# Layer A's attention on Trainium2: the value products of near, block and selected keys in one batch per tile and group

## The chip, the cores and the metric

The kernel runs on one core of a Trainium2 chip. The metric is the device time of one execution in microseconds. Three runs of the kernel before took 2791.73, 2793.88 and 2795.78 us; the median is 2793.88 us. Times inside the kernel come from one profiled execution, counted from the start of its span. PE is TensorE, DVE is VectorE, ACT is ScalarE, POOL is GpSimd, SP is SyncE, which issues DMAs.

## The reference, cut to what matters

The program is a two-layer decoder trunk on 1024 tokens of width 1024. Layer A's attention has 16 heads in 4 groups; the 4 heads of a group share their keys and values. Each query attends three sets of keys, and the three results are added under gates:

```python
s = einsum('bsgrd,bngd->bgrsn', q, k_cmp) * scale          # 63 compressed blocks
p, denom, _ = masked_softmax(s + bias_c, dist_c >= 0)
p_cmp = p / maximum(denom, 1e-30)
o_cmp = einsum('bgrsn,bngd->bsgrd', p_cmp, v_cmp)
_, sel_idx = top_k(score, 8)                               # 8 of 16 key blocks, from p_cmp
...
o_sel = einsum('bcgrk,bgckd->bcgrd', p_sel / den, vg)      # the selected blocks alone
o_win, _ = banded_attention(q, kwn, vwn, 255, 1, rel_bias) # the last 256 keys
o = g[..., 0:1] * o_cmp + g[..., 1:2] * o_sel + g[..., 2:3] * o_win
```

Everything is float32. Layer B's dilated attention, the projections and the feed-forward parts are not edited, apart from one call in layer B whose arguments become fewer.

## The kernel before, in words

The stage in question is layer A's attention; its value products stand in the trace from 286 to 673 us of 2792. Its unit of work is one group `g` (4 of them) and one tile `t` of 128 queries (8 of them): 32 units, taken group by group. For one unit:

- `near_scores` (called `a` for two heads and `b` for the other two) multiplies queries by the keys of the tile and of two tiles before it and by the 63 compressed keys (line 758), and DVE adds the bias, takes the minimum and moves the scores from PSUM to SBUF (lines 759 and 761, weights in the tiles `P2` and `pc`). `block_weights` (`c`) turns the compressed scores into weights and, for t of 4 and more, into the mask of selected blocks, which `block_mask` (`m`) turns with PE (line 813).
- `far_scores` (`f`, `g`, two heads each) does the same for all keys up to the tile (lines 845 to 847), in tiles `P1` of 128 x 2 x 1024 numbers, of which there are 4. `exponentials` runs the exponential on ACT (line 738), the reciprocal on DVE (740) and the scaling by sum and gate on POOL (742).
- `near_values` (`n`) and `far_values` (`v`) multiply weights by values. A weight tile has the queries on its partitions, so PE turns it first: `turned` makes four 128 x 128 transposes into a PSUM bank `pt` (line 353; three such banks) and ACT or DVE, in turn, copies the bank to a tile `pT` (line 356; 5 such tiles). A product then has 64 columns of values as PE's weights and 256 turned columns as the moving side; two heads' products go to two halves of PE's columns (line 390). For 128 keys ("a block") that is two products, which the profile shows as four records, since each float32 product runs as two.

The helper `values` does this for a list of blocks in batches of at most 3: it turns up to 3 blocks, and then does their products, last block first, with `after(prev)` so that the products stand behind the last transpose on PE. `near_values` calls it for 1 to 3 near blocks and appends the product of the compressed keys to the batch; `far_values` calls it for the t + 1 blocks of the selected keys, in 1 to 3 batches. Both add into the same half bank `o` in PSUM, which `po_` hands from one to the other; DVE then copies it to `oT` (line 860).

`turn(i)` sets the order of steps in the source: a(i+2), m(i), f(i), v(i-1), b(i+2), c(i+2), n(i), g(i). The language's scheduler reorders from there what does not depend on each other, so that on PE scores of later units stand between transposes and products of earlier ones.

Of the kernel before, what the change touches and what calls it, by code (L numbers as in the profile page):

```python
# [10 lines left out]
F32 = mybir.dt.float32  # L11
# [118 lines left out]
def trunk(ctx, tc, I, out):  # L130
    nc = tc.nc
# [74 lines left out]
    def after(prev):  # L206
        return tc.issue_after(prev.ins) if prev is not None else ExitStack()
# [141 lines left out]
    def turned(p, heads, copy):  # L349

        ps = bank("pt")
        for i, h in enumerate(heads):
            prev = nc.tensor.transpose(ps[:, i * 128:(i + 1) * 128], h, ident)  # L353
        w = len(heads) * 128
        t = p.tile([128, 512], F32, name="pT", bufs=5)
        copy(t[:, :w], ps[:, :w])  # L356
        return t, prev

# [7 lines left out]
            self.i += 1  # L366
            return self.parts[(self.i - 1) % len(self.parts)]

    copies = [0]

    def values(p, po, Ps, vs, first, last, behind=None, more=None):

        nb = len(vs)
        ends = [nb * (i + 1) // -(-nb // 3) for i in range(-(-nb // 3))]
        for lo, hi in zip([0] + ends, ends):
            ts = []
            for b in range(lo, hi):
                copies[0] += 1  # L380
                t, prev = turned(p, [Ps[hp][:, e, b * 128:(b + 1) * 128] for e in range(2) for hp in range(2)],
                                 (nc.scalar.copy, nc.vector.tensor_copy)[copies[0] % 2])
                ts.append(t)
            ops = [(vs[b], vs[b], ts[b - lo][:, :256], ts[b - lo][:, 256:]) for b in reversed(range(lo, hi))]
            if more is not None and lo == 0:
                ops.append(more)
            for i, (*v, ta, tb) in enumerate(ops):
                with after(prev), after(behind if lo == i == 0 else None):
                    for e, t in enumerate((ta, tb)):
                        mm = nc.tensor.matmul(po[64 * e:64 * e + 64, :256], v[e], t, start=first and lo == i == 0,  # L390
                                              stop=last and hi == nb and i == len(ops) - 1, skip_group_check=True)
                prev = mm
        return prev

    def pipelined(jobs, lag=1):

# [26 lines left out]
    vc = ares.tile([128, G, 128], F32, name="vc")  # L423
# [4 lines left out]
    with ExitStack() as c:  # L428
# [62 lines left out]
        with ExitStack() as c2:  # L491
# [14 lines left out]
            first = [xget(t) for t in range(4)]  # L506
# [12 lines left out]
            prev = norm_to_hT(np_, xget, g_mix[0], *hT, 4, 4)  # L519
# [147 lines left out]
        grp = {}  # L667
# [55 lines left out]

        pcs = [kP.tile([128, 4, 64], F32, name=f"pc{i}") for i in range(3)]
        units = [(g, t) for g in range(G) for t in range(NT)]
        po_, blocks_, weights = {}, {}, {}
        first_banks = Turns(("cmp0", "cmp1"))
        score_bank = lambda: psum["s"].tile([128, 512], F32, name="s", bufs=4) if "s" in psum else bank(first_banks())
        gt = lambda g, t, br, h0, n: gates[:, t, 12 * g + 3 * h0 + br:12 * g + 3 * (h0 + n):3]
# [47 lines left out]
        def block_weights(g, t):  # L777
            pc, pv, mx, nv = blocks_[g, t]
            dn = kP.tile([128, 4], F32, name="cd", bufs=3)
            for hh in range(4):  # L780
                nc.scalar.activation(pc[:, hh, :nv], pc[:, hh, :nv], AF.Exp, bias=mx[:, hh:hh + 1], scale=-1.0,
                                     accum_out=dn[:, hh:hh + 1])
            nc.vector.tensor_scalar(dn, dn, 1e-30, None, op0=OP.max)
            nc.vector.reciprocal(dn, dn)
            if t == 0:
                nc.vector.tensor_scalar(dn, dn, crow, None, op0=OP.mult)
            dg = kP.tile([128, 4], F32, name="dg", bufs=3)
            nc.vector.tensor_mul(dg, dn, gt(g, t, 0, 0, 4))
            if t >= 4:
                pn = wk.tile([128, 4, 64], F32, name="pn", bufs=2)  # L790
                nc.gpsimd.tensor_mul(pn[:, :, :nv], pv, dn[:].unsqueeze(2).to_broadcast([128, 4, nv]))
            nc.gpsimd.tensor_mul(pv, pv, dg[:].unsqueeze(2).to_broadcast([128, 4, nv]))
            if t >= 4:
                a4 = wk.tile([128, 68], F32, name="a4", bufs=2)
                nc.gpsimd.memset(a4, 0.0)
                nc.vector.tensor_reduce(a4[:, 1:1 + nv], pn[:, :, :nv].rearrange("p h n -> p n h"), axis=AX.X,
                                        op=OP.add)
                sc = wk.tile([128, 16], F32, name="sc", bufs=2)
                nc.vector.tensor_reduce(sc, a4[:, 1:65].rearrange("p (j i) -> p j i", i=4), axis=AX.X, op=OP.add)
                nc.vector.tensor_add(sc, sc, a4[:, 0:64].rearrange("p (j i) -> p j i", i=4)[:, :, 0])  # L800
                nc.vector.tensor_add(sc, sc, force[:, t, :])
                m8 = wk.tile([128, 8], F32, name="m8", bufs=2)
                nc.vector.max(out=m8, in_=sc)
                s2_ = wk.tile([128, 16], F32, name="s2", bufs=2)
                nc.vector.match_replace(out=s2_, in_to_replace=m8, in_values=sc, imm_value=-3e38)
                mk = wk.tile([128, 16], F32, name="mk", bufs=2)
                nc.vector.tensor_scalar(mk, s2_, -2e38, BIG, op0=OP.is_gt, op1=OP.mult)
                grp["mask", g, t] = mk
# [8 lines left out]
        def near_values(g, t):  # L817
            pc = blocks_[g, t][0]
            pT, _ = turned(wk, [pc[:, 2 * c:2 * c + 2, :] for c in range(2)], nc.vector.tensor_copy)
            po = po_[g, t] = outs()  # L820
            k0 = max(t - 2, 0)
            ends[0] = values(wk, po, grp["P2", g, t], [grp["V", 1, g, b // 4][:, b % 4, :] for b in range(k0, t + 1)],
                             True, False, ends[0], (vc[:, g, :64], vc[:, g, 64:], pT[:, :256], pT[:, :256]))

        def far_scores(g, t, hp):

            n = 128 * (t + 1)
            P = weights[1, hp] = wk.tile([128, 2, 1024], F32, name="P1", bufs=4)
            mm = kP.tile([128, 2], F32, name="m", bufs=8)
            masked = t >= 4  # L830
            kh, kl = grp["K", g]
# [22 lines left out]
                grp["P1", g, t] = weights[1, 0], weights[1, 1]  # L854

        def far_values(g, t):
            po = po_[g, t]
            ends[0] = values(wk, po, grp["P1", g, t], [grp["V", 0, g, b // 4][:, b % 4, :] for b in range(t + 1)],
                             False, True)
            nc.vector.tensor_copy(oT[:, 2 * g:2 * g + 2, tok(t)], po.rearrange("p (c q) -> p c q", q=128))  # L860

        def loads(g, t):
# [51 lines left out]
    with ExitStack() as c:  # L914
        kB = pool(c, "aB")
        wk = pool(c, "aw")
# [759 lines left out]
    oT_ctx, bctx = ExitStack(), ExitStack()  # L1676
    oT = pool(oT_ctx, "oTb", "left").tile([128, KC, S], F32, name="oTb")
    bC, bA = pool(bctx, "bC", "right"), pool(bctx, "bA", "right")
    with ExitStack() as c:
        wk = pool(c, "bw")  # L1680
        bB = pool(c, "bB")
# [75 lines left out]
        def unit(key, hp, stats, slot, score, bias, n, blocks, dst):  # L1757
# [15 lines left out]
            def back():  # L1773
                if hp == 0:
                    return
                po = outs()
                behind[0] = values(wk, po, both, blocks, True, True, behind[0])
                nc.vector.tensor_copy(dst, po[:, :256].rearrange("p (c q) -> p c q", q=128))
            return back

# [184 lines left out]
```

## Time and profile before

| what | value |
|---|---|
| median of the runs | 2793.88 us |
| span of the profiled execution | 2792.1 us |
| PE busy over the span | 2738.9 us (98%) |
| DVE, ACT, POOL busy over the span | 79%, 51%, 50% |
| layer A's attention, 286 to 672 us: PE busy | 376.31 of 386 us |
| there: DVE, ACT, POOL busy | 316.45, 279.32, 217.59 us |
| granted TensorE clock there | 1.00 |

The profiled execution's span is 1.8 us under the median of the runs and inside their spread. Its busy figures are sums of the stretches in which an engine has an instruction under way. Matmuls are pipelined and their ends are modelled, so two starts on PE tell more than a duration and a gap. A wait of an engine is put down to the semaphore that came last.

### The profile page before, as it was taken

The page shows a single profiled execution, that of the slowest core. Times are in us where ns is not written, and L with a number is a line of the kernel's source. Part 1 is how long each engine was busy: PE and PEld are TensorE (multiplying, and loading weights), DVE is VectorE, ACT ScalarE, POOL GpSimd, SP SyncE. Part 2 cuts the span into 40 slices and gives each one's busy share as a digit, 9 for nine tenths or more (in the row PEclk, how much of TensorE's full clock was granted, in tenths as well). Part 3 has the DMA queues.
Part 4 walks back from the last instruction along what each step waited for, and adds up shares of the span by engine and source line. Part 5 has one row for each costly group of instructions (what it writes and reads, how often), then busy time and mean ns, then how long its engine had stood idle before and what let it go on. Part 6 is the DMA issues. An engine that isn't in the chain of part 4 may idle for free.

```text
span 2792.1 us, 43025 instructions
## 1 busy us (share of the span) xinstructions
PE 2738.9 (98%) x14494; PEld 2218.9 (79%) x14494; DVE 2214.7 (79%) x4527; ACT 1426.8 (51%) x3171; POOL 1402.8 (50%) x1454
## 2 busy tenths in 40 slices
PE   9999999999999999999999999999999999999997
PEld 8988676776788888888778888777778888888886
DVE  5453888887889899989875677688898888888987
ACT  5531777775644343333454444577756433343434
POOL 3135655552465566565457787110014756655652
PEclk9999999999999999999999999999999999999999
DMA  8669443224122322232224555786341211112112
GB/s 237 218 196 298 133 128 105 68 62 159 35 76 69 83 65 68 62 77 62 84 80 116 167 156 159 242 257 187 114 174 44 74 58 57 49 57 61 54 42 83
DMA packets 292924, 315.13 MB, mean 113 GB/s; under 512 B 50428, under 2 KB 229677, under 8 KB 292704
## 3 DMA queue, kind: packets, MB, share of 16 engines
q1 hardware_dynamic: 272240, 249.40, 30.5%
q0 software_dynamic: 20464, 62.99, 7.4%
q8 instruction: 115, 1.88, 0.3%
q14 instruction: 105, 0.86, 0.1%
HBM read 243.96 MB, written 81.95 MB: 117 GB/s over the span
## 4 chain that ended last, share of the span: by engine, by line
PE 85%; DVE 6%; ACT 2%; issue 2%; DMA 2%; POOL 1%; SPq 1%; POOLq 0%; DVEq 0%; ACTq 0%
PE ux L1161 18%; PE uy L1161 15%; PE dx L993 8%; PE o L390 7%; PE pt L353 6%; PE dr L993 6%; PE dr L1161 4%; PE mm L230 3%; PE mm L229 3%; PE mm L231 3%; PE s L758 1%; DVE pl L954 1%; PE s L846 1%; PE s L1808 1%; PE s L845 1%
## 5 line engine op out<-in xcount | busy, mean ns | idle before, releaser
L954 DVE TENSOR_TENSOR pl<-oT,ph 128x512 fp32r<-128x512 f32 x340 | 340.2, 1018 | 72.3 <-PE dr L993 17.4
L953 ACT ACTIVATE ph<-oT 128x512 fp32r<-128x512 f32 x346 | 211.8, 628 | 215.6 <-PE ux L1161 53.3
L954 DVE TENSOR_TENSOR pl<-oTb,ph 128x512 fp32r<-128x512 f32 x232 | 214.7, 948 | 27.2 <-PE dr L993 17.4
L953 ACT ACTIVATE ph<-oTb 128x512 fp32r<-128x512 f32 x238 | 145.5, 628 | 168.7 <-PE ux L1161 53.4
L353 PE MATMUL pt<-ident,P 128*128 128x128 f32 x1536 | 228.0, 278 | 3.3 <-DVE pT L356 1.9
L742 POOL TENSOR_SCALAR P<-P,sm,gates 128x384 f32<-128x384 f32 (+7 forms) x256 | 183.2, 727 | 79.3 <-DVE sm L740 54.8
L353 PEld LDWEIGHTS pt<-ident,P 128*128 128x128 f32 x1536 | 172.9, 140 | 61.8 <-issue 43.0
L998 DVE TENSOR_TENSOR xrfx<-xrfx,dr 128x512 f32<-128x512 f32 x320 | 204.2, 679 | 17.8 <-PE dr L993 17.7
L1354 POOL TENSOR_TENSOR oT<-oT,gffn 128x512 f32<-128x512 f32 x92 | 118.9, 1303 | 196.0 <-DMA oT<-in_ffn_w_up_dram 127.7
L998 DVE TENSOR_TENSOR xrfx<-xrfx,dx 128x512 f32<-128x512 f32 x320 | 204.5, 678 | 2.2 <-PE dx L993 2.2
L738 ACT ACTIVATE P<-P,m 128x384 f32<-128x384 f32 (+7 forms) x256 | 171.1, 670 | 36.0 <-DVE m L851 14.9
L356 DVE COPY pT<-pt 128x512 f32<-128x512 f32 (+1 forms) x224 | 143.2, 648 | 44.5 <-PE pt L353 39.8
L1354 POOL TENSOR_TENSOR oTb<-oTb,gffn 128x512 f32<-128x512 f32 x92 | 111.8, 1226 | 130.8 <-DMA oTb<-in_ffn_w_up_dram 79.0
L356 ACT COPY pT<-pt 128x512 f32<-128x512 f32 x192 | 110.1, 578 | 103.8 <-PE pt L353 100.8
L390 PE MATMUL o<-pT,V 128*64 128x256 f32 x1200 | 160.7, 391 | 2.3 <-ACT pT L356 1.5
L1770 ACT ACTIVATE P<-P,st 128x384 f32<-128x384 f32 (+2 forms) x256 | 139.6, 548 | 32.3 <-DVE st L1765 30.4
L1765 DVE CUSTOM_DVE_ANT_0 P<-s,T 128x384 f32<-128x384 f32 (+2 forms) x256 | 112.9, 478 | 10.5 <-PE pt L353 3.0
L390 PEld LDWEIGHTS o<-pT,V 128*64 128x64 f32 x1200 | 73.6, 136 | 51.8 <-issue 9.9
L993 PE MATMUL dx<-ph 128*128 128x512 f32 x320 | 107.5, 390 | 0.8 <-ACT ph L953 0.8
L993 PE MATMUL dx<-ph,pl 128*128 128x512 f32 x320 | 107.0, 389 | 0.0
L847 DVE CUSTOM_DVE_ANT_0 P<-s,T 128x128 f32<-128x128 f32 (+3 forms) x192 | 99.5, 550 | 8.1 <-PE s L846 7.8
L230 PE MATMUL mm<-hL,wh 128*128 128x512 f32 (+1 forms) x272 | 102.6, 378 | 0.0
(623 smaller groups left out, 8040.3 us busy)
## 6 DMA issues: line engine op xcount, KB each, us to landing
qB<-xrfx POOLq DMA_DIRECT2D x96, 256.0 KB, 4.5
oT<-in_ffn_w_up_dram SPq DMA_DIRECT2D x92, 256.0 KB, 2.9
oTb<-in_ffn_w_up_dram SPq DMA_DIRECT2D x92, 256.0 KB, 2.9
Q<-qB SPq DMA_DIRECT2D x40, 512.0 KB, 6.9
wd<-in_ffn_w_down_dram SPq DMA_DIRECT2D x60, 256.0 KB, 2.6
oT<-in_b_w_q_dram SPq DMA_DIRECT2D x48, 256.0 KB, 5.6
K<-kBs SPq DMA_DIRECT2D x40, 256.0 KB, 7.5
wraw<-in_a_w_in_dram SPq DMA_DIRECT2D x18, 512.0 KB, 6.9
```

The costliest lines, as they stand in the source:

```text
L230: nc.tensor.matmul(ps, lh, rl, start=False, stop=False, skip_group_check=bool(shared))
L353: prev = nc.tensor.transpose(ps[:, i * 128:(i + 1) * 128], h, ident)
L356: copy(t[:, :w], ps[:, :w])
L390: mm = nc.tensor.matmul(po[64 * e:64 * e + 64, :256], v[e], t, start=first and lo == i == 0, stop=last and hi == nb and i == len(ops) - 1, ...
L738: nc.scalar.activation(P[:, e, :n], P[:, e, :n], AF.Exp, bias=mm[:, e:e + 1], scale=-1.0, accum_out=sm[:, e:e + 1])
L742: nc.gpsimd.tensor_scalar(P[:, e, :n], P[:, e, :n], sm[:, e:e + 1], gate(e), op0=OP.mult, op1=OP.mult)
L953: nc.scalar.activation(h, src, AF.Copy)
L954: self.last = (eng or nc.vector).tensor_sub(l, src, f32(h))
L993: nc.tensor.matmul(banks[t], part(a, t)[u], b[v], start=z == 0 and onX != 2, stop=z == 2, skip_group_check=True)
L998: nc.vector.tensor_add(xs, xs, banks[t])
L1161: mm = nc.tensor.matmul(b, x[:, i * 128:(i + 1) * 128], ys[i], start=first and (z, i) == (0, 0), stop=(z, i) == (2, 3), skip_group_check=True)
L1354: nc.gpsimd.tensor_mul(v, v, gains[:, k:k + 4].unsqueeze(2).to_broadcast([128, 4, 128]))
```

## The change

`values` is cut in two. `turn_blocks` turns all blocks of a list and returns the products still to be done; `chained` does a list of products behind the last transpose. In layer A `near_values` now only turns its blocks and keeps the products in `near_`; `far_values` turns all t + 1 blocks and then does the products of selected, near and compressed keys as one batch, which starts with the last two selected blocks. So there is one batch per unit. Layer B calls the new `values`, which turns and multiplies in one batch the 2 or 3 blocks that it had in one batch before.

The turned tiles `pT` must live longer: there are 11 in layer A (8 selected and 3 near) and again 5 in layer B. The turned compressed weights have a tile `pH` of their own. To make room, the tiles `P1` of selected weights go from 4 to 3, and `pn` from 2 to 1.

```diff
-        t = p.tile([128, 512], F32, name="pT", bufs=5)
+        t = p.tile([128, 512], F32, name="pT", bufs=pt_bufs[0]) if w == 512 else \
+            p.tile([128, 256], F32, name="pH", bufs=1)
...
-    def values(p, po, Ps, vs, first, last, behind=None, more=None):
...
+    def turn_blocks(p, Ps, vs):
+
+        ops = []
+        for b, v in enumerate(vs):
+            copies[0] += 1
+            t, prev = turned(p, [Ps[hp][:, e, b * 128:(b + 1) * 128] for e in range(2) for hp in range(2)],
+                             (nc.scalar.copy, nc.vector.tensor_copy)[copies[0] % 2])
+            ops.append((v, v, t[:, :256], t[:, 256:]))
+        return ops, prev
+
+    def chained(po, ops, prev, behind=None):
+
+        for i, (*v, ta, tb) in enumerate(ops):
+            with after(prev), after(behind if i == 0 else None):
+                for e, t in enumerate((ta, tb)):
+                    mm = nc.tensor.matmul(po[64 * e:64 * e + 64, :256], v[e], t, start=i == 0,
+                                          stop=i == len(ops) - 1, skip_group_check=True)
+            prev = mm
         return prev
...
-                pn = wk.tile([128, 4, 64], F32, name="pn", bufs=2)
+                pn = wk.tile([128, 4, 64], F32, name="pn", bufs=1)
...
-            ends[0] = values(wk, po, grp["P2", g, t], [grp["V", 1, g, b // 4][:, b % 4, :] for b in range(k0, t + 1)],
-                             True, False, ends[0], (vc[:, g, :64], vc[:, g, 64:], pT[:, :256], pT[:, :256]))
+            ops, _ = turn_blocks(wk, grp["P2", g, t], [grp["V", 1, g, b // 4][:, b % 4, :] for b in range(k0, t + 1)])
+            near_[g, t] = [(vc[:, g, :64], vc[:, g, 64:], pT[:, :256], pT[:, :256])] + ops
...
-            P = weights[1, hp] = wk.tile([128, 2, 1024], F32, name="P1", bufs=4)
+            P = weights[1, hp] = wk.tile([128, 2, 1024], F32, name="P1", bufs=3)
...
-            po = po_[g, t]
-            ends[0] = values(wk, po, grp["P1", g, t], [grp["V", 0, g, b // 4][:, b % 4, :] for b in range(t + 1)],
-                             False, True)
+            po = outs()
+            ops, prev = turn_blocks(wk, grp["P1", g, t], [grp["V", 0, g, b // 4][:, b % 4, :] for b in range(t + 1)])
+            ends[0] = chained(po, ops[-2:][::-1] + near_[g, t] + ops[:-2], prev, ends[0])
```

The first place is PE in the second group, where the unit t = 6 gets its selected values. `s` are scores of later steps, `pt` banks of transposes, `o` the products, `P1`, `P2` and `pc` the weights of selected, near and compressed keys. Before, two blocks are multiplied between the transposes of two others:

```order
L353 MATMUL pt_5716<-ident_67,P1_5590 128x128
L845 MATMUL s_5810<-K2_3004,Q13_4321 128x512
L846 MATMUL s_5810<-K3_3005,QM0_4323 128x512
L390 MATMUL o_2871<-pT_5703,V2_3010 64x256 x2
L390 MATMUL o_2871<-pT_5696,V2_3010 64x256 x2
L353 MATMUL pt_5723<-ident_67,P1_5446 128x128
L353 MATMUL pt_5723<-ident_67,P1_5590 128x128
```

Of the change, the same unit's eleven blocks stand in one row, seven selected, the compressed and three near:

```order
L387 MATMUL o_2871<-pT_5712,V0_4331 64x256 x2
L387 MATMUL o_2871<-pT_5705,V0_4331 64x256 x2
L387 MATMUL o_2871<-pH_5559,vc_92 64x256 x2
L387 MATMUL o_2871<-pT_5566,VW10_4317 64x256 x2
L387 MATMUL o_2871<-pT_5573,VW10_4317 64x256 x2
L387 MATMUL o_2871<-pT_5580,VW10_4317 64x256 x2
L387 MATMUL o_2871<-pT_5670,V2_3006 64x256 x2
L387 MATMUL o_2871<-pT_5677,V2_3006 64x256 x2
L387 MATMUL o_2871<-pT_5684,V2_3006 64x256 x2
L387 MATMUL o_2871<-pT_5691,V2_3006 64x256 x2
L387 MATMUL o_2871<-pT_5698,V0_4331 64x256 x2
L353 MATMUL pt_5784<-ident_67,P20_5206 128x128
```

The products of this unit have moved to one place behind its last transposes. Over layer A's attention the order of PE holds 107 separate stretches of products before and 37 of the change (32 units, five of which the scheduler cuts once); the products and the transposes are the same in number.

The second place is PE where the near values of that unit were made. Before, the four products of the near and compressed keys stand right behind their transposes:

```order
L353 MATMUL pt_5575<-ident_67,P25_5101 128x128
L813 MATMUL pt_5644<-ident_67,mk_5348 16x128
L353 MATMUL pt_5673<-ident_67,P1_5446 128x128
L845 MATMUL s_5658<-K2_3004,Q11_4317 128x512
L390 MATMUL o_2871<-pT_5580,VW10_4325 64x256 x2
L390 MATMUL o_2871<-pT_5573,VW10_4325 64x256 x2
L390 MATMUL o_2871<-pT_5566,VW10_4325 64x256 x2
L390 MATMUL o_2871<-pT_5559,vc_92 64x256 x2
L353 MATMUL pt_5680<-ident_67,P1_5446 128x128
```

Of the change, scores and mask follow the near transposes, and no product:

```order
L353 MATMUL pt_5575<-ident_67,P25_5101 128x128
L846 MATMUL s_5597<-K2_3000,Q13_4313 128x512
L847 MATMUL s_5597<-K3_3001,QM0_4315 128x512
L760 MATMUL s_5620<-KW4_5407,Q00_4991 128x320
L760 MATMUL s_5620<-KW5_5408,Q00_4991 128x320
L760 MATMUL s_5625<-KW4_5407,Q01_4993 128x320
L760 MATMUL s_5625<-KW5_5408,Q01_4993 128x320
L815 MATMUL pt_5636<-ident_67,mk_5348 16x128
L846 MATMUL s_5642<-K2_3000,Q10_4307 128x512
```

What filled PE there before, 4 blocks of products, now stands later.

The third place is DVE at the same time, where it begins the second `P1` tile of the next unit, t = 7. `P1_...<-s_...` moves one score tile, `pT` and `pH` are copies of turned banks. The semaphores that an instruction waits for stand in brackets. Before:

```order
L847 ISA P1_5799,mp_5801<-s_5802,T2_4333 128x512 [waits PE_49,Pool_49]
L847 ISA mp_5801 128x1
L847 ISA P1_5799,mp_5801<-s_5806,T10_3150 128x512 [waits PE_49]
L847 ISA mp_5801 128x1
L356 COPY pT_5714<-pt_5709 128x512 [waits PE_49]
L847 ISA P1_5799,mp_5801<-s_5810,T3_4336 128x512 [waits PE_49]
L847 ISA mp_5801 128x1
L740 RECIPROCAL sm_5667<-sm_5667 128x2 [waits Activation_49]
L356 COPY pT_5728<-pt_5723 128x512 [waits DVE_49,PE_49]
```

Of the change:

```order
L357 COPY pT_5698<-pt_5693 128x512 [waits PE_49]
L848 ISA P1_5791,mp_5793<-s_5794,T2_4325 128x512 [waits PE_49,Pool_49]
L848 ISA mp_5793 128x1
L848 ISA P1_5791,mp_5793<-s_5798,T10_3144 128x512
L848 ISA mp_5793 128x1
L357 COPY pT_5712<-pt_5707 128x512 [waits PE_49]
L848 ISA P1_5791,mp_5793<-s_5802,T3_4328 128x512
L848 ISA mp_5793 128x1
```

With three `P1` tiles, `P1_5791` takes the place of `P1_5438`, the first weights of unit t = 6, so its first row has to wait until PE has turned the last block of that unit; the rows behind it wait for nothing more from PE. Before, with four, `P1_5799` took the place of a tile of unit t = 5, and each of its rows waited for its own scores alone.

More of the change, by code (lines that the diff above doesn't have):

```diff
@@ L367, in __call__, with values @@
             return self.parts[(self.i - 1) % len(self.parts)]
-    copies = [0]
-    def values(p, po, Ps, vs, first, last, behind=None, more=None):
[L375 to L392, printed above, removed]
-        return prev
+    copies, pt_bufs = [0], [11]
+    def turn_blocks(p, Ps, vs):
[13 more added lines that the diff above has]
+            prev = mm
+        return prev
+    def values(p, po, Ps, vs, behind=None):
+        ops, prev = turn_blocks(p, Ps, vs)
+        return chained(po, ops[::-1], prev, behind)
     def pipelined(jobs, lag=1):
@@ L725, in trunk @@
         units = [(g, t) for g in range(G) for t in range(NT)]
-        po_, blocks_, weights = {}, {}, {}
+        near_, blocks_, weights = {}, {}, {}
         first_banks = Turns(("cmp0", "cmp1"))
@@ L819, in near_values @@
             pT, _ = turned(wk, [pc[:, 2 * c:2 * c + 2, :] for c in range(2)], nc.vector.tensor_copy)
-            po = po_[g, t] = outs()
             k0 = max(t - 2, 0)
-            ends[0] = values(wk, po, grp["P2", g, t], [grp["V", 1, g, b // 4][:, b % 4, :] for b in range(k0, t + 1)],
-                             True, False, ends[0], (vc[:, g, :64], vc[:, g, 64:], pT[:, :256], pT[:, :256]))
+            ops, _ = turn_blocks(wk, grp["P2", g, t], [grp["V", 1, g, b // 4][:, b % 4, :] for b in range(k0, t + 1)])
+            near_[g, t] = [(vc[:, g, :64], vc[:, g, 64:], pT[:, :256], pT[:, :256])] + ops
         def far_scores(g, t, hp):
             n = 128 * (t + 1)
-            P = weights[1, hp] = wk.tile([128, 2, 1024], F32, name="P1", bufs=4)
+            P = weights[1, hp] = wk.tile([128, 2, 1024], F32, name="P1", bufs=3)
             mm = kP.tile([128, 2], F32, name="m", bufs=8)
@@ L1678, in trunk @@
     bC, bA = pool(bctx, "bC", "right"), pool(bctx, "bA", "right")
+    pt_bufs[0] = 5
     with ExitStack() as c:
@@ L1776, in back @@
                 po = outs()
-                behind[0] = values(wk, po, both, blocks, True, True, behind[0])
+                behind[0] = values(wk, po, both, blocks, behind[0])
                 nc.vector.tensor_copy(dst, po[:, :256].rearrange("p (c q) -> p c q", q=128))
```

## The prediction, as put on record

> **What bounds the kernel now.** I read the page's busy times first, then the busy time of each engine by stage, the groups of instructions inside layer A's attention, PE's timeline there, and last the waits of that stage. First the page's span, and the table by stage: the whole attention, then two groups of heads, each cut in a first half (units t = 0 to 4) and a second (t = 5 to 7). Its columns are PE, PE's weight loads, DVE, ACT and POOL, busy us with the count of instructions.
>
> ```profile
> span 2792.1 us, 43025 instructions
> ```
>
> ```profile
> core 0: us, PE busy (x) PEld busy (x) DVE busy (x) ACT busy (x) POOL busy (x), PEclk, DMA share, GB/s
> 286.00:672.00 386.00, 376.31 (x2640) 269.17 (x2640) 316.45 (x1411) 279.32 (x867) 217.59 (x379) 1.00 0.35 99
> 390.00:440.00 50.00, 49.39 (x345) 36.03 (x342) 45.88 (x216) 40.01 (x131) 31.54 (x55) 1.00 0.25 70
> 440.00:487.00 47.00, 46.36 (x327) 32.11 (x327) 34.84 (x154) 31.47 (x98) 24.88 (x47) 1.00 0.50 135
> 487.00:537.00 50.00, 49.61 (x344) 35.77 (x343) 46.47 (x216) 39.79 (x130) 31.18 (x54) 1.00 0.25 70
> 537.00:583.00 46.00, 45.06 (x331) 33.07 (x330) 34.60 (x152) 31.55 (x100) 22.41 (x39) 1.00 0.37 97
> ```
>
> PE bounds the stage: 376.31 of 386 us, at a granted clock of 1.00 throughout. DVE is second, and unevenly: in first halves it rests 4.1 and 3.5 of 50 us, in second halves 12.2 and 11.4 of 47 and 46. So PE time that the change frees is worth its full price in second halves, and in first halves only as long as DVE keeps up.
>
> What PE does in the stage, by groups (busy us, mean ns of one; products are the lines L390, transposes L353):
>
> ```profile
> L353 PE MATMUL pt<-ident,P 128*128 128x128 f32 x908 | 138.0, 279 | 3.3 <-DVE pT L356 1.9 <-ACT pT L356 1.1
> L390 PE MATMUL o<-pT,V 128*64 128x256 f32 x576 | 79.1, 392 | 2.1 <-ACT pT L356 1.5 <-DVE pT L356 0.4
> L390 PE MATMUL o<-pT,VW 128*64 128x256 f32 x336 | 43.3, 389 | 2.3 <-ACT pT L356 1.3 <-DVE pT L356 0.8
> L390 PE MATMUL o<-pT,vc 128*64 128x256 f32 x128 | 19.2, 379 | 0.0
> ```
>
> That is 576 + 336 + 128 = 1040 records of products, four a block. Their shape is 128*64, half of PE's columns, where transposes and scores have 128*128. The change removes none of them. What it removes is switches between the two shapes, so the question is what a switch costs. PE's timeline shows it (start, length, count of records):
>
> ```profile
> 574.15 0.60 PE L353 MATMUL pt<-ident,P 128*128 128x128 f32 x4
> 574.68 1.08 PE L390 MATMUL o<-pT,V 128*64 128x256 f32 x8
> 575.69 1.53 PE L353 MATMUL pt<-ident,P 128*128 128x128 f32 x12
> 577.15 1.51 PE L390 MATMUL o<-pT,V 128*64 128x256 f32 x12
> 578.60 0.66 PE L353 MATMUL pt<-ident,P 128*128 128x128 f32 x4
> ...
> 593.58 0.65 PE L390 MATMUL o<-pT,V 128*64 128x256 f32 x4
> 594.17 0.66 PE L353 MATMUL pt<-ident,P 128*128 128x128 f32 x4
> 594.75 0.65 PE L390 MATMUL o<-pT,V 128*64 128x256 f32 x4
> ```
>
> From start to start, 8 products take 575.69 - 574.68 = 1.01 us and 12 take 578.60 - 577.15 = 1.45, so one more costs 0.44 / 4 = 0.11. Of transposes between two batches, 12 take 577.15 - 575.69 = 1.46 and 4 take 594.75 - 594.17 = 0.58, so one more costs 0.88 / 8 = 0.11. A full round of 4 products and 4 transposes takes 594.75 - 593.58 = 1.17 where the work alone is 8 x 0.11 = 0.88. The remaining **0.29 us is the price of a batch**, into the half-width shape and out again. PE loses it with no wait on any engine.
>
> **The change part by part.** *Fewer batches.* In PE's order the attention has 107 stretches of products before and 37 after, 70 fewer. The source gives 92 and 32 (8 near and 15 far batches a group, then 8); the scheduler cuts 15 and 5 more. 70 x 0.29 = 20.3 us less PE work. [...]
>
> *Scores in new places.* Longer runs of transposes are broken by scores more often (150 changes from transposes to scores in the order, 131 before). That costs nothing, by this stretch:
>
> ```profile
> 641.31 0.66 PE L353 MATMUL pt<-ident,P 128*128 128x128 f32 x4
> 641.72 0.94 PE L845 MATMUL s<-K,Q 128*128 128x512 f32 x3
> 642.50 0.38 PE L353 MATMUL pt<-ident,pc 128*128 128x128 f32 x2
> 642.63 0.48 PE L845 MATMUL s<-K,Q 128*128 128x512 f32 x1
> 642.95 0.60 PE L353 MATMUL pt<-ident,P 128*128 128x128 f32 x4
> ```
>
> Six transposes and four scores take 642.95 - 641.31 = 1.64 us. The transposes are 6 x 0.11 = 0.66, which leaves 0.245 a score, against 0.26 in the three that follow each other (0.78 / 3). There are three changes of kind in it and no room for a price.
>
> *Products that wait for copies.* Each batch waits for the copy of its last block. PE's and its weight loads' waits in the stage:
>
> ```profile
> PEld o L390 <- ACT pT L356: 6.7, 17, 0.9
> PEld pt L353 <- DVE pT L356: 4.3, 10, 0.9
> PEld o L390 <- DVE pT L356: 3.6, 10, 0.6
> PE o L390 <- ACT pT L356: 2.8, 6, 0.7
> PE o L390 <- DVE pT L356: 1.2, 5, 0.3
> ```
>
> PE itself lost 2.8 + 1.2 = 4.0 us this way in 107 batches. At the same rate 37 lose 1.4, so 2.6 us go. What comes in their place is the wait of a transpose for a free bank. Up to 8 blocks are now turned with no product between, into three banks, and each must be copied out first. The two copies, and for the next step DVE's reduction of one score tile:
>
> ```profile
> L356 DVE COPY pT<-pt 128x512 f32<-128x512 f32 x114 | 77.2, 686 | 25.9 <-PE pt L353 23.6 <-PE o L390 1.1
> L356 ACT COPY pT<-pt 128x512 f32<-128x512 f32 x114 | 65.2, 579 | 74.8 <-PE pt L353 73.0 <-PE o L390 1.6
> L847 DVE CUSTOM_DVE_ANT_0 P<-s,T 128x512 f32<-128x512 f32 x96 | 64.2, 684 | 6.0 <-PE s L846 5.9
> ```
>
> Four transposes take 0.44 us, and two engines in turn empty a bank every 0.686 / 2 = 0.34 if both are free, every 0.69 if one does it alone. So it holds while DVE isn't inside its own score work, and slips when it is. All of PE's work stands behind a transpose that waits. A bank wait took 4.3 / 10 = 0.43 us above. I put one more such wait on each unit of t = 5 to 7, 12 x 0.43 = 5.2 us. The bounds are none, and one on each of the 32 units, 13.8.
>
> *DVE in the first halves.* About 33 of the 70 batches lie there, 33 x 0.29 = 9.6 us, 2.4 a half. For PE to get them, DVE would have to be busy 45.88 of 47.6 us, 96%. But while PE multiplies it makes no scores, and now it multiplies a unit's 3, 5, 7, 8 and 9 blocks (t = 0 to 4) at a stretch: 32 blocks of 4 records at 0.11, 14.1 us a half. What DVE can have in hand at the start of a batch is four score tiles and some copies, 4 x 0.684 + 0.686 = 3.4 us if all banks are full, and they seldom are. With two thirds of each batch covered it rests 4.7 us a half, more than the 4.1 and 3.5 of now. So I give the 9.6 us back in full. The bounds are none of it and, with half of each batch covered (7 us of rest, 3 more than now in each of four halves), 9.6 + 12 = 21.6.
>
> *Three `P1` tiles.* The second pair of heads of a unit may be reduced into `P1` only when PE has turned all selected weights of the unit before. That closes a ring: reductions, exponentials, scaling, transposes, reductions. Its rows for t = 7 (the reduction's stands above), and the copies of `o` that end two units:
>
> ```profile
> L738 ACT ACTIVATION_READ_ACCUMULATOR P<-P,m 128x1 f32 x247 | 47.1, 190 | 0.0
> L742 POOL TENSOR_SCALAR P<-P,sm,gates 128x1024 f32<-128x1024 f32 x16 | 19.0, 1199 | 15.2 <-DVE sm L740 15.2
> L738 ACT ACTIVATE P<-P,m 128x1024 f32<-128x1024 f32 x16 | 18.3, 1146 | 3.3 <-DVE m L851 3.2
> ```
>
> ```profile
> 470.75 0.42 DVE L860 COPY oT<-o 128x256 f32<-128x256 f32 x1 [1.34 <-PE o L390]
> 486.84 0.42 DVE L860 COPY oT<-o 128x256 f32<-128x256 f32 x1
> ```
>
> 4 x 0.684 + 2 x (1.146 + 0.190) + 2 x 1.199 + 32 x 0.11 = 11.3 us, against 486.84 - 470.75 = 16.1 a unit. It fits with 4.8 to spare, so I price it at nothing. Queued behind the waiting reduction on DVE are copies of turned blocks, which PE needs; the rival below prices that.
>
> *The rest.* One `pn`: it is used once a unit and free long before the next. One `pH`: DVE's copy into it waits for the third block of the batch of the unit before; behind it on DVE stands the copy of `o`, which waits for that batch's end anyway. Both cost nothing. Layer B's order is the same, and its products stay in one batch a unit. At the stage's end the next stage's loads start when the last scores are done, as before; its first instructions are ordered a little differently with no work added.
>
> *Sum.* -20.3 - 2.6 + 5.2 + 9.6 = -8.1 us. From the span of 2792.1 that gives 2784.0; the median of the runs lies 1.8 above the span, so **2786 us**.
>
> **The rivals.** *A, all of it:* nothing new waits; 2792.1 - 22.9 + 1.8 = 2771.0. For it: DVE rests 316.45 against 386, and 365 would still hold it. Against: the first halves.
>
> *B, no change:* PE gets its 20 us but alternates with DVE and ACT. Long runs of transposes and products leave DVE without scores; a long run of scores after them makes PE wait for DVE. Price: in first halves the 9.6 us go as in the forecast, and bank waits on all 32 units take 13.8; 2792.1 - 22.9 + 23.4 + 1.8 = 2794.4. For it: before, products filled the time in which weights pass ACT and POOL, and now transposes of the same unit stand there. Against: near scores run two units ahead and can fill in. [...]
>
> *C, slower:* the ring of three `P1` tiles. On each unit the reductions wait, and then each of two exponentials stands behind a copy on ACT (0.579), 1.2 us a unit. The ring is long only from t = 2 on, 24 units: 28.8 us; 2792.1 - 20.3 + 28.8 + 1.8 = 2802. It decides once a unit loses over 20.3 / 32 = 0.63 us, and it is slower by 0.2% once it loses 0.81. Against: 4.8 us to spare at t = 7. For: the waiting reduction heads DVE's queue, with copies behind it that PE needs.
>
> **How the numbers follow.** A measurement of this kernel tells 0.2%, 5.6 us, from no change: under 2788.3 is faster, over 2799.5 slower. I give the forecast 0.50: with one of its two give-backs at half or at half as much again it runs from 2779 to 2791, and of the 0.50 I put 0.42 under 2788.3 and 0.08 above. A has 0.14, B 0.20, C 0.16. Faster 0.42 + 0.14 = 0.56, same 0.08 + 0.20 = 0.28, slower 0.16. The range goes from A to a little beyond B, 2771 to 2800, and leaves out most of C.
>
> **What would show it.** Right: PE busy in the attention falls by 16 to 20 us from 376.31, the stage by 8 from 386; the busy time of L390's products falls, and a batch of 8 blocks still costs 0.11 a record; the first half of a group stays near 50 us with DVE's rest near 4, and the second falls from 47 to about 45. Half right: the first halves shorten too (A), or waits of transposes on pT copies grow past 5 us (B). Wrong: reductions into `P1` (DVE P L847) that wait 0.6 us a unit and more for transposes, or a stage no shorter than 386 us.

## The result and the profile after

The changed kernel takes 2818.24 us (median of 5 runs, 2817.69 to 2823.83) against 2793.88 (5 runs, 2791.73 to 2797.10): ratio 1.0088, 95% interval 1.0076 to 1.0099. It is slower by some 24 us, outside the predicted range and on the other side of no change. The profiled execution spans 2815.9 us, 23.8 more than before.

The table by stage (columns as in the prediction): the attention, and the two halves of group 1.

```profile
286.00:700.00 414.00, 379.71 (x2645) 279.20 (x2645) 319.79 (x1413) 282.37 (x868) 216.11 (x379) 0.98 0.32 92
404.00:458.00 54.00, 50.83 (x336) 36.10 (x336) 47.91 (x217) 38.57 (x123) 30.44 (x54) 0.97 0.23 65
458.00:508.00 50.00, 44.80 (x332) 33.42 (x331) 34.99 (x150) 32.75 (x101) 25.34 (x47) 1.00 0.46 124
```

The attention now ends near 699 instead of 673 us: all of the loss lies in it. PE's busy time rose by 3 us, but the stage grew by 26, so PE now idles some 34 us in it where it idled 10. The first half of this group, which the prediction wanted near 50 us, takes 54, and the second, which it wanted at 45, takes 50. And the granted clock, 1.00 throughout before, is 0.98. The groups of PE in the stage:

```profile
L353 PE MATMUL pt<-ident,P 128*128 128x128 f32 x908 | 136.5, 281 | 20.1 <-POOL P L744 14.0 <-DVE pT L357 5.6
...
L387 PE MATMUL o<-pT,V 128*64 128x256 f32 x576 | 75.3, 389 | 2.4 <-DVE pT L357 1.6 <-ACT pT L357 0.7
...
L387 PE MATMUL o<-pT,VW 128*64 128x256 f32 x336 | 41.7, 379 | 0.0
...
L387 PE MATMUL o<-pH,vc 128*64 128x256 f32 x128 | 19.5, 384 | 0.0
```

The products got cheaper (79.1 to 75.3, 43.3 to 41.7; all products together keep PE busy for 121.5 us where it was 135.9). PE's busy time rose all the same, because its scores got dearer. The stage by the same columns with the score tiles `s` alone, before and after:

```profile
286.00:673.00 387.00, 150.36 (x614) 100.03 (x614) 173.98 (x476) 0.00 (x0) 0.00 (x0) 1.00 0.35 100
286.00:699.00 413.00, 163.23 (x614) 99.06 (x613) 174.50 (x475) 0.00 (x0) 0.00 (x0) 0.98 0.32 91
```

The same 614 records take 163.2 us in place of 150.4. The idle time ahead of transposes of weights went from 3.3 to 20.1 us, and 14.0 of it ends with POOL's scaling of the weights, line 744. Before, POOL stood in no row of that group. PE's and its weight loads' waits say the same, and show the smaller ones on DVE:

```profile
PEld pt L353 <- POOL P L744: 19.5, 19, 3.2
...
PE pt L353 <- POOL P L744: 14.0, 10, 2.9
...
PE pt L353 <- DVE pT L357: 7.3, 11, 1.3
PEld s L760 <- DVE mp L848: 5.3, 16, 1.0
...
PEld s L846 <- DVE mp L848: 5.0, 13, 1.0
```

Why POOL is late shows in the timeline at the end of group 0 (start, length, and in brackets the idle time before it with its releaser). POOL, then what its scaling needs from DVE, SP's loads of the bias, and PE:

```profile
370.08 0.51 POOL L691 TENSOR_SCALAR_AFFINE_SELECT TW<-T 128x384 f32<-128x384 f32 x1 [6.85 <-DMA T<-sA]
370.58 2.15 POOL L744 TENSOR_SCALAR P<-P,sm,gates 128x896 f32<-128x896 f32 x2
...
383.03 0.23 POOL L696 COPY C<-T 128x31 f32<-128x31 f32 x1 [4.82 <-DMA T<-sA]
383.70 0.51 POOL L691 TENSOR_SCALAR_AFFINE_SELECT TW<-T 128x384 f32<-128x384 f32 x1 [0.45 <-DMA T<-sA]
...
386.11 2.37 POOL L744 TENSOR_SCALAR P<-P,sm,gates 128x1024 f32<-128x1024 f32 x2
...
378.01 0.69 DVE L848 CUSTOM_DVE_ANT_0 P<-s,T 128x512 f32<-128x512 f32 x1
...
382.21 0.17 DVE L742 RECIPROCAL sm<-sm 128x2 f32<-128x2 f32 x1 [2.50 <-ACT P L740]
...
378.96 3.56 SPq L687 DMA_DIRECT2D T<-sA  x5
...
384.03 0.38 PE L353 MATMUL pt<-ident,P 128*128 128x128 f32 x2
387.36 1.76 PE L353 MATMUL pt<-ident,P 128*128 128x128 f32 x7 [2.94 <-POOL P L744]
```

The last weights of t = 7 are ready to be scaled at 382.38, when DVE's reciprocal ends. POOL starts on them at 386.11, 3.7 us later: copies and selects on the *next* group's bias stand ahead of them in its queue, and for 2.0 of the 3.7 us (0.65, 0.45 and 0.89) POOL idles on their transfers. PE waits 2.94 us for the first tile. These copies are not new, and neither are their waits; the waits are fewer (16 where there were 19) and longer. POOL's waits on the bias transfers, before and after:

```profile
POOL C L694 <- DMA T<-sA: 13.4, 12, 3.1
POOL TW L689 <- DMA T<-sA: 11.3, 7, 3.6
```

```profile
POOL C L696 <- DMA T<-sA: 20.3, 9, 5.5
...
POOL TW L691 <- DMA T<-sA: 18.8, 7, 7.1
```

24.7 us before and 39.1 after. The transfers themselves start late: the five at 378.96 go out 0.26 us after the last score reduction of t = 7 ends (378.01 + 0.69), and those reductions read the bias tiles whose slots are to be filled again. So there is a loop: the reductions wait for a `P1` tile, the bias load for the reductions, POOL's copy for the load, the scaling for the copy, the transposes for the scaling, and a `P1` tile comes free when the transposes are done. It closes at the ends of groups, where the bias changes: PE's waits on POOL there are 2.94 us at 387, 1.73 at 495 and 2.22 at 592.

In this wait of 2.94 us PE's granted clock falls too. Stretches from 386 us, by the columns of the table by stage (the clock stands third from the end):

```profile
386.00:388.00 2.00, 0.65 (x3) 0.65 (x4) 0.00 (x0) 0.81 (x5) 2.00 (x3) 0.64 0.00 1
...
390.00:392.00 2.00, 2.00 (x10) 1.91 (x9) 1.95 (x11) 1.89 (x7) 0.66 (x2) 0.50 0.00 0
392.00:394.00 2.00, 2.00 (x12) 1.81 (x12) 0.39 (x2) 0.97 (x5) 1.50 (x4) 0.66 0.34 112
```

Taking each row as a mix of 1.0 and 0.5, the clock is at 0.5 from 386.5 to 393.4 us. Two more such stretches, from 314.9 and from 451.4, last 3.4 us each. At 0.5 a score of 256 columns starts 0.21 us after the one before it (391.26 to 391.47), at 1.00 it was 0.12 (383.67 to 383.79). So in 13.6 us at half clock PE loses at most 6.8; for a part of them it stands still anyway.

### The profile page after: what moved, and what is told of

Its sections match the earlier page's. It is cut to its first block, busy times and chain, and to the rows that moved or that the text cites. A ratio compares the mean times of both kernels' runs of the same rounds, so it can differ in the third digit from the quotient of the medians.

```text
span 2815.9 us, 42926 instructions
## 1 busy us (share of the span) xinstructions
PE 2741.9 (97%) x14494; PEld 2230.8 (79%) x14494; DVE 2222.8 (79%) x4527; ACT 1426.6 (51%) x3171; POOL 1400.0 (50%) x1454
## 4 chain that ended last, share of the span: by engine, by line
PE 82%; DVE 7%; DMA 3%; ACT 3%; POOL 2%; issue 2%; SPq 1%; POOLq 0%; DVEq 0%; ACTq 0%
PE ux L1162 18%; PE uy L1162 14%; PE dx L994 8%; PE dr L994 5%; PE o L387 5%; PE pt L353 5%; PE dr L1162 4%; PE mm L229 3%; PE mm L230 3%; PE mm L231 3%; PE dx L1162 1%; PE s L1810 1%; ACT P L740 1%; DVE pl L955 1%; PE s L1790 1%
## 5 line engine op out<-in xcount | busy, mean ns | idle before, releaser
L353 PE MATMUL pt<-ident,P 128*128 128x128 f32 x1536 | 226.4, 279 | 20.1 <-POOL P L744 14.0
L357 DVE COPY pT<-pt 128x512 f32<-128x512 f32 x192 | 130.8, 687 | 29.9 <-PE pt L353 27.4
L229 PE MATMUL mm<-hH,wh 128*128 128x512 f32 (+1 forms) x272 | 102.8, 380 | 0.0
```

Of the source, the lines that this page charges most:

```text
L229: nc.tensor.matmul(ps, lh, rh, start=first, stop=False, skip_group_check=bool(shared))
```

## The experiments

To compare runs taken at different times, the us behind each name below are its ratio to the kernel before, less one, times 2793.9. The changed kernel is at +24.6 in this measure. An interval of the ratio is about 0.1% wide to each side, 3 to 4 us. The scheduler orders each kernel anew, so twins differ a little in order too: PE has 107 stretches of products in the kernel before, 110 in `p1_three_only` and 103 in `p1_three_held`.

**The ring alone, and batches with four tiles.** Theory 1 was the ring of three `P1` tiles, theory 2 the long batch itself. `p1_three_only` is the kernel before with

```diff
-            P = weights[1, hp] = wk.tile([128, 2, 1024], F32, name="P1", bufs=4)
+            P = weights[1, hp] = wk.tile([128, 2, 1024], F32, name="P1", bufs=3)
```

> The kernel before with one number changed: the ring of P1 tiles has three instead of four. Batches, order of products and the ring of turned tiles stay as they were (110 stretches of products in PE's order, 107 before). Theory 1, the ring of three P1 tiles is what costs the time: slower by 15 to 30 us, 2809 to 2824, with PE's waits of transposes on POOL's scaling (P) grown from about 1 us to over 15. Theory 2, the long lump of transposes and products costs the time and the ring has time to spare: within 5 us of before, those waits under 5 us. Theory 3, both are needed together: in this order other products fill the time, so 2 to 10 us slower.

Measured: 2823.09 us, 1.0101 (1.0086 to 1.0117), **+28**. This one number costs more than the whole change, as theory 1 expected in size. Its sign, over 15 us of PE's waits on POOL's scaling, didn't come: PE's row has 7.1. The trace has the same picture, with the same copy in the way (POOL, then PE):

```profile
383.13 0.23 POOL L694 COPY C<-T 128x31 f32<-128x31 f32 x1 [2.31 <-DMA T<-sA]
...
384.56 2.38 POOL L742 TENSOR_SCALAR P<-P,sm,gates 128x1024 f32<-128x1024 f32 x2
...
385.81 2.18 PE L353 MATMUL pt<-ident,P 128*128 128x128 f32 x9 [3.82 <-POOL P L742]
```

No run has four `P1` tiles and eleven turned ones together. `hybrid_p3` and `hybrid_p4` take seven turned tiles and cut long units in two:

```diff
-            ops, prev = turn_blocks(wk, grp["P1", g, t], [grp["V", 0, g, b // 4][:, b % 4, :] for b in range(t + 1)])
-            ends[0] = chained(po, ops[-2:][::-1] + near_[g, t] + ops[:-2], prev, ends[0])
...
+            cut = nb if t < 4 else 4
+            for lo, hi in ((0, cut), (cut, nb)):
...
+                ops = ops[-2:][::-1] + (near_[g, t] if lo == 0 else []) + ops[:-2]
+                ends[0] = chained(po, ops, prev, ends[0] if lo == 0 else None, first=lo == 0, last=hi == nb)
```

> The changed kernel with seven turned tiles in place of eleven: units t = 0 to 3 in one batch as there, units t = 4 to 7 in two (four far blocks with the near ones and the block weights, then the rest). Three P1 tiles. 58 stretches of products in PE's order. It is the twin of the next kernel. Theory 1 (ring): 49 fewer batches at 0.29 us give 14 us back and the ring costs what it costs in the changed kernel, some 40 us, less what the first batch's earlier start spares: 2805 to 2820. Theory 2 (lump): the lump is cut for the long units, so between before and the changed kernel, 2795 to 2810.

> The same kernel as the one before it with four P1 tiles instead of three and nothing else changed; 60 stretches of products. Theory 1 (ring): the waits on POOL's scaling go, what is left is 47 fewer batches at 0.29 us, -14 us, and some 5 us of transposes waiting for banks: 2780 to 2790, faster than before, and 20 us and more under its twin. Theory 2 (lump): within 5 us of its twin, and slower than before.

`far_one_p4` keeps the near batch of before at its place, with the turned compressed weights in a `pT` tile again, and joins only the selected blocks (`cut = nb if t < 7 else 4`), with four `P1` tiles.

> Four P1 tiles as before and the near batch with the block weights at its old place; only the far products of a unit go in one batch (two at t = 7), with seven turned tiles. 68 stretches of products, 39 fewer than before. Theory 1 (ring): -39 x 0.29 = -11 us with a few us of bank waits against it, 2782 to 2790. Theory 2 (lump): the near products still fill in, but the far lump starves DVE of scores: 2794 to 2805.

Measured: `hybrid_p3` 2832.43, 1.0138 (1.0122 to 1.0153), **+39**; `hybrid_p4` 2817.94, 1.0085 (1.0070 to 1.0100), **+24**; `far_one_p4` 2799.85, 1.0019 (1.0008 to 1.0029), **+5**. The fourth tile is worth 15 us between the twins, so the ring counts, but theory 1 alone falls: `hybrid_p4` has it and is no faster than the changed kernel. Theory 2 alone falls with `p1_three_only`.

**POOL's queue.** In these four traces most of PE's long waits on POOL stand near the changes of groups, beside POOL's waits for the bias (the longest of `hybrid_p3` doesn't; it follows below). This gives a new theory 3, POOL's queue; the theory 3 of the first expectation, that ring and batch cost only together, fell with `p1_three_only`. The next kernels put the selects and copies off until the products just recorded are done:

```diff
+                if hold:
+                    held.append(work)
...
+                if what == 'v' and held:
+                    with waiting(ends[0]):
+                        while held:
+                            held.pop(0)()
```

where `work` holds the affine_select and the tensor_copy of `load_bias`; the loads stay where they were, and group 0's own bias isn't held.

> The changed kernel, with POOL's work on the bias of the next group (the selects into TW and the copies into C) held until the products of the unit then finished are done, so that none of it stands ahead of the scaling of a long unit's weights while its own DMA is still under way. Ring of three, lump of products and everything else as in the changed kernel. Theory 3, POOL's queue held up by those transfers lengthens the ring at the ends of the groups: PE's waits on POOL's scaling at the ends of groups 0 to 2 (2.9, 1.7, 2.2 us and smaller ones) go, and most of the stretches at clock 0.5 with them: 2798 to 2808. Theory 1, the ring is too short by itself: within 5 us of the changed kernel, 2813 to 2822.

> Four P1 tiles, one batch a unit up to t = 3 and two from t = 4, and POOL's bias work held as in after_held. Theory 3: with the ring at four and POOL free the saving of some 47 batches at 0.29 us is left with the bank waits against it, 2782 to 2795. Theory 2, the lump itself: near products no longer fill the time in which weights are made, so still 2805 and more.

> far_one_p4 (2799.9 us) with POOL's bias work held as in after_held. Theory 3: the two or three waits of PE on POOL's scaling at the ends of groups (2.6, 0.4, 2.0 us) go with the two stretches at clock 0.5: 2786 to 2794, so at or under the kernel before. Otherwise 2797 to 2803.

> The kernel before with POOL's bias work held in the same way and nothing else changed: the control. There the scaled weights had time to spare (0.6 us of PE's waits on them in all), so every theory expects 2788 to 2798. Much slower would mean that holding costs something by itself, and the other three would have to be read against that.

Measured: `after_held` 2798.89, 1.0011 (1.0001 to 1.0020), **+3**; `hybrid_p4_held` 2806.43, 1.0038 (1.0023 to 1.0053), **+11**; `far_one_p4_held` 2795.08, 1.0000 (0.9990 to 1.0009), **0**; `before_held` 2794.15, 0.9997 (0.9988 to 1.0006), **-1**. So 21 of the 25 us of the changed kernel go, and the control doesn't move: the same POOL work in the same place costs nothing that the runs show in the kernel before (-1 us when it is held), where the waits on POOL's scaling come to one row, 0.6 us of PE's weight loads. Holding also takes 13 us off `hybrid_p4` and 5 off `far_one_p4`, which have four `P1` tiles, so the short ring isn't all that lays POOL's queue bare; joined products do it too. And `hybrid_p4_held` stays at +11, in the range that its expectation gave to the long batch itself. In `after_held` POOL goes from one scaling to the next, and the bias copies come when the last products of the group are done:

```profile
371.63 3.44 POOL L752 TENSOR_SCALAR P<-P,sm,gates 128x1024 f32<-128x1024 f32 x4 [3.25 <-DVE m L860]
...
375.31 2.37 POOL L752 TENSOR_SCALAR P<-P,sm,gates 128x1024 f32<-128x1024 f32 x2
...
390.03 0.75 POOL L701 COPY C<-T 128x31 f32<-128x31 f32 x4
```

Its PE waits, in the rows of above, are these:

```profile
PEld pt L353 <- DVE pT L357: 12.6, 24, 1.2
...
PE pt L353 <- DVE pT L357: 6.0, 10, 1.0
PEld s L854 <- DVE mp L856: 5.1, 13, 1.0
PEld pt L353 <- POOL P L752: 5.0, 9, 2.1
PEld s L768 <- DVE mp L856: 5.0, 16, 1.0
...
PE pt L353 <- POOL P L752: 2.1, 2, 1.8
```

PE's waits on POOL fall from 14.0 to 2.1 us; those on DVE stay (6.0 against 7.3, 5.1 and 5.0 against 5.0 and 5.3). One short stretch of lowered clock is left, 3.4 us from 631.5.

**The ring without POOL's waits.** `p1_three_held` is `p1_three_only`, and `hybrid_p3_held` is `hybrid_p3`, with the bias work held.

> p1_three_only (2823.1 us: the kernel before with three P1 tiles) with POOL's bias work held as in after_held, and nothing else. Theory 3, a ring of three has time to spare as long as POOL scales at once, and what lengthens it is POOL waiting for the bias transfers: the 30 us go all but a few, 2793 to 2801. Theory 1, three tiles cost by themselves: half or more of the 30 us stays, 2808 to 2825.

> hybrid_p3 (2832.4 us) with POOL's bias work held; the twin of hybrid_p4_held (2806.4 us) with three P1 tiles instead of four. Theory 3 alone (the ring of three costs only through POOL's waits): within 4 us of the twin, 2803 to 2811. Theory 1 beside it (the ring of three costs by itself as well, as p1_three_held says with some 15 us in the old order): 2815 to 2824.

Measured: `p1_three_held` 2809.34, 1.0051 (1.0036 to 1.0066), **+14**; `hybrid_p3_held` 2815.92, 1.0082 (1.0067 to 1.0097), **+23**, 12 over its twin with four tiles. About half of what three tiles cost in the old order goes with POOL's waits (28 to 14) and half stays; theory 3 isn't the whole of the ring. In `p1_three_held` PE's waits are spread over copies and reductions. On DVE, though, the ring stands out: its reductions into `P1` wait for PE's transposes,

```profile
DVE P L855 <- PE pt L353: 17.8, 18, 1.8
```

against 15.5 us in `p1_three_only`, 12.1 in `hybrid_p3` and 10.4 in `hybrid_p3_held`; the kernel before and the hybrids with four tiles have no such row. The end of the last group in `hybrid_p3`, where no bias is left to load, shows one turn of the ring (DVE, POOL, PE):

```profile
684.44 0.69 DVE L848 CUSTOM_DVE_ANT_0 P<-s,T 128x512 f32<-128x512 f32 x1 [2.83 <-PE pt L353]
...
691.77 2.38 POOL L744 TENSOR_SCALAR P<-P,sm,gates 128x1024 f32<-128x1024 f32 x2 [7.61 <-DVE sm L742]
...
693.03 0.88 PE L353 MATMUL pt<-ident,P 128*128 128x128 f32 x6 [3.51 <-POOL P L744]
```

The reduction waits 2.8 us for transposes of the unit before. PE can turn the new weights 8.6 us after the reduction starts, and has stood still for the last 3.5 of them. In the changed kernel itself such waits of DVE come to 3.8 us only, and in `after_held` to 4.5.

**Joining the near products.** `near_joined_p4_held` keeps selected blocks in batches of up to three and adds the near ones to the first (`if lo == 0: ops = near_[g, t] + ops`), four `P1` tiles, seven turned ones, bias work held.

> Four P1 tiles, POOL's bias work held, far products in batches of up to three as before; the near products and the block weights join the first far batch. 73 stretches of products, 34 fewer than before, -10 us. If the joining by itself takes away the work that fills PE while weights pass ACT and POOL: 2797 to 2808, slower than far_one_p4_held (2795.1 us) with about as many batches. If only long runs of turning starve DVE: 2788 to 2795.

Measured: 2810.96, 1.0065 (1.0050 to 1.0080), **+18**, against 0 of `far_one_p4_held` with about as many stretches of products (73 and 72). In these two forms it is the joining that costs, not the long batch. But `after_held` joins as well, and is at +3; what differs is that it has eleven turned tiles, where in `near_joined_p4_held` waiting near tiles hold up to three of seven. That wasn't taken apart.

**DVE's load.** What `after_held` still waits for is mostly DVE. Theory 4: with two of three copies on ACT instead of one of two, that shrinks.

```diff
-                             (nc.scalar.copy, nc.vector.tensor_copy)[copies[0] % 2])
+                             (nc.scalar.copy, nc.vector.tensor_copy)[copies[0] % mix[0] == 1])
```

with `mix[0] = 3` in layer A and 2, as before, in layer B.

> after_held (2798.9 us) with ACT making two of three copies of turned tiles in layer A's attention instead of one of two; DVE loses some 38 copies of 0.68 us, ACT gets them at 0.58. Theory 4, what still eats the 20 us of saved batches is DVE: PE's transposes and scores wait for its copies and reductions, 24 us in the stage in after_held. Then a third of that goes: 2787 to 2794, and under the kernel before. Against it: ACT's exponentials stand behind its copies and the weights come later, so 2797 to 2806.

> far_one_p4_held (2795.1 us) with the same shift of copies from DVE to ACT. Theory 4: PE's waits on DVE there are some 11 us, a third goes, 2788 to 2793, which would be the fastest. Against it: 2794 to 2802.

> The control for the shift: before_held (2794.2 us) with two of three copies on ACT. There PE waits on DVE for 9 us and on ACT for 4. Theory 4 expects little, 2790 to 2796; if ACT is the tighter engine here, 2797 to 2803.

> The changed kernel with two of three copies of turned tiles on ACT and POOL's bias work where the change left it (not held). If the two causes, POOL's queue and DVE's load, add up: 2818 - 9 = 2809 (2805 to 2813). If the shift matters only once POOL is out of the way: 2814 to 2822. If the lighter DVE frees the tiles of the bias sooner and so mends POOL's waits as well: under 2803.

Measured: `after_held_act` 2790.12, 0.9987 (0.9978 to 0.9997), **-4**, 7 less than without the shift; `far_one_p4_held_act` 2785.51, 0.9969 (0.9958 to 0.9981), **-9**, 9 less; `before_held_act` 2800.04, 1.0023 (1.0013 to 1.0032), **+6**, 7 more; `after_act` 2805.40, 1.0045 (1.0028 to 1.0062), **+13**, 12 less than the changed kernel. The same shift helps wherever products were joined and hurts the kernel before. Holding and shifting add up to within 5 us: 21 and 12 one by one, 28 together. The copies and PE's waits on DVE in `after_held_act`:

```profile
L357 ACT COPY pT<-pt 128x512 f32<-128x512 f32 x152 | 84.5, 581 | 56.1 <-PE pt L353 55.3
...
L357 DVE COPY pT<-pt 128x512 f32<-128x512 f32 x76 | 52.1, 685 | 14.7 <-PE pt L353 14.4
```

```profile
PEld pt L353 <- DVE pT L357: 6.4, 14, 0.8
...
PE pt L353 <- DVE pT L357: 2.8, 6, 0.6
```

The transposes' wait for DVE's copies halves (6.0 to 2.8 on PE, 12.6 to 6.4 on its weight loads), as theory 4 has it. `far_one_p4_held_act` is the fastest kernel found, 0.3% under the one before.

## Why the prediction was wrong

*The price of a batch* was right. From start to start, less the 0.109 us of a transpose and 0.1075 of a product, the median change from products to transposes costs 0.20 us in both traces, and one into products 0.09. The first were counted 99 times before and 35 after, the second 107 and 37: 64 x 0.20 + 70 x 0.09 = 19 us, where I had 20.3. One batch of the changed kernel, in which 44 products start within 491.88 - 486.99 = 4.89 us, 0.111 each with the way out:

```profile
486.99 1.08 PE L387 MATMUL o<-pT,V 128*64 128x256 f32 x8
487.90 0.60 PE L387 MATMUL o<-pH,vc 128*64 128x256 f32 x4
488.33 1.47 PE L387 MATMUL o<-pT,VW 128*64 128x256 f32 x12
489.63 2.33 PE L387 MATMUL o<-pT,V 128*64 128x256 f32 x20
491.88 0.66 PE L353 MATMUL pt<-ident,P 128*128 128x128 f32 x4
```

*Products that wait for copies* were right in direction and a little under size: 4.0 us before; the product rows above have 2.4, so 1.6 went where I had 2.6.

*Bank waits of transposes*, 5.2 us, were right: PE's wait on DVE's copies rose from 1.9 to 7.3, by 5.4 (by 4.3 net, since 1.1 us on ACT's copies went).

*What DVE gives back*, 9.6 us, came out in size, though not only in first halves. From start to start PE loses 3.6 us to DVE's minima of scores before (its tiles cm, mp and m, waits over 0.15 us) and 13.5 in `after_held`, 9.9 more. Since a third less copying on DVE takes 7 us off `after_held`, DVE's load as a cause is shown by that run.

*Scores in new places*, priced at nothing, is a term that failed. The changes from transposes to scores and back did stay free, to within 2 us. What rose is the work of the scores themselves: PE's busy time on them went from 150.4 to 163.2 us, and is still 161.5 in `after_held`. From start to start, without waits over 0.15 us and without the lowered clock, steps from one score to the next lose 12.7 us before (against the usual step of their shape, 0.232 us for 128x512), 21.5 in the changed kernel and 22.5 in `after_held`, so 9 to 10 more. For some 4 of them the last thing waited for is DVE; for most of the rest the profile names no wait, and the cause stays open. So the sign of PE busy 16 to 20 us lower failed: products fell by 14.3, and scores rose by 12.9.

*Three `P1` tiles, priced at nothing*, is the step that failed most. I added the durations on the ring, 11.3 us, held them against a unit of 16.1, and took the 4.8 between them for room. The runs put the ring at +28 us alone in the old order and at 15 between the hybrids. A sum of durations leaves out how long each step waits for its engine. Half of that is POOL's, which I had counted only with its scalings: its queue holds the next group's selects and copies, behind which a scaling started 3.7 us after its inputs were there, and their waits on transfers, 24.7 us before, looked harmless since PE's weight loads waited 0.6 us for it. With three tiles or with joined products PE has nothing else to turn in that time; which of the two weighs more in the changed kernel wasn't told apart. The other half (14 us in `p1_three_held`, 12 between the hybrids held) is the ring itself. The sign that I gave for it, reductions that wait 0.6 us a unit for transposes, comes in `p1_three_held` (17.8 / 32 = 0.56), but not in the changed kernel (3.8 / 32 = 0.12), whose loss shows in the waits on POOL and in a stage longer than 386 us. How DVE's waits reach PE there stays open.

*Rival C* had the sign and the ring, and the wrong place. It set 1.2 us on 24 units and came to 2802. The waits come in a few lumps, most at the ends of groups, 2.9 us in one, through an engine that it didn't name. Its reason, the waiting reduction at the head of DVE's queue, is what `p1_three_held` shows, with 17.8 us of such waits. *Rival B* is close to `after_held`: 2794.4 with nothing left of the saving, measured 2798.89.

*The clock* was in no term. The stretches at half clock come with the other waits: 13.6 us of them in the changed kernel, 3.4 in `after_held`. By the profiled spans, holding the bias work is worth 2815.9 - 2797.1 = 18.8 us. PE's waits on POOL over 0.15 us fell by 13.3 from start to start (16.3 to 3.0). The remaining 5.5 are of the size of what the clock gives back, at most 5.1.

So the sum of the changed kernel reads: -19 of batches, -2 of products' waits, +5 of banks, +10 of DVE's scores, +9 of scores after scores, +21 through POOL's queue with the lowered clock in it, together +24 of the +25 measured. The terms were read from the traces; of them POOL's queue, and DVE's load in part, were tested by runs. What three tiles cost by themselves in the changed kernel's own order lies inside these terms; no run tried it with a fourth. The single `pH`, priced at nothing, wasn't tried alone either; DVE waits 5.3 us for it, in 12 waits.

Two slips in the prediction carry nothing: with one give-back at half, the forecast's lower end is 2781 and not 2779, and the stretch at 641 us has four changes of kind, not three.

## What to carry to other kernels

Before a ring of buffers is shortened, list everything that stands in each queue of the ring, work of other stages and its transfers too, and ask for each wait in it whom it would hold then; a sum of durations against the period shows only that the ring can close. When work is moved, price what it does to the work it lands beside, here scores after scores. If a trade of buffers for fewer switches fails, try what is in the way one by one: putting off POOL's foreign work and moving a sixth of the copies to ACT turned +25 us into -4 without touching the change itself. A shift of load between engines has to be tried in the order in which it will run, since the same one cost the kernel before 7 us.

## What the runs showed of the hardware

The length of PE's last wait alone doesn't tell whether its granted clock falls. In the timeline above PE's last transposes before the wait end at 384.41, the clock is at 0.5 from 386.5 on, 2.1 us later, and it stays there for 6.8 us though PE works again from 387.36. After single waits of 1.73 us at 495 and 2.22 at 592 it stays at 1.00 (488 to 500 and 585 to 600 us). Around 451 us no single wait of PE is longer than 0.79 us, three within 4 us, and the clock still goes to 0.5 for 3.4 us:

```profile
448.00 0.66 PE L353 MATMUL pt<-ident,P 128*128 128x128 f32 x4 [0.47 <-DVE pT L357]
449.44 0.66 PE L353 MATMUL pt<-ident,P 128*128 128x128 f32 x4 [0.78 <-DVE pT L357]
...
451.11 0.57 PE L760 MATMUL s<-KW,Q 128*128 128x256 f32 x2 [0.79 <-DVE mp L848]
```

```profile
452.00:456.00 4.00, 4.00 (x25) 2.30 (x25) 2.59 (x10) 1.95 (x4) 0.71 (x3) 0.65 0.00 0
```

So two stretches at 0.5 came after waits of 2.67 us (it ended at 313.81) and 2.94, one after three waits of under 0.8, and the waits of 1.73 and 2.22 had none behind them. The three stretches in the attention last 3.4, 6.8 and 3.4 us. What makes the clock fall isn't shown by these runs.
